# Where the steps of the next layer's modulation stand among the early gate projections

## The chip, the cores and the metric

The kernel runs on one core of a Trainium2 chip. The metric is the device time of one execution in microseconds (us). Engines are named as the profile names them: PE does matrix multiplications (PEld its weight loads), DVE is the vector engine, ACT the scalar engine with its activation functions, POOL the general engine, and SP issues most transfers. Each engine, and each queue of transfers, takes its instructions in one fixed order.

## The reference

A trunk of two layers over 512 tokens of width 1024, all in float32. Each layer:

```python
mod = c_act @ w_ada[l] + b_ada[l]              # 3072 values from one condition vector
shift, scale, gate = split(mod, 3)
h = rms_norm(x, g_pre[l]) * (1 + scale) + shift
cq, ckv, kr, za, qb, kb, vb, zb, qc, kc, vc, zc, gcols = split(h @ w_in[l])
o_a = (mla(cq, ckv, kr) * silu(za)) @ w_o_mla[l]       # low-rank attention, 8 heads
o_b = (swa(qb, kb, vb) * silu(zb)) @ w_o_swa[l]        # sliding window, 8 heads, sinks
o_c = (diff(qc, kc, vc) * silu(zc)) @ w_o_diff[l]      # differential attention, 4 heads
g = sigmoid(gcols)                                     # 3 branches x 1024
y = (g[0] * o_a + g[1] * o_b + g[2] * o_c) @ w_out[l]
x = x + gate * rms_norm(y, g_post[l])
```

The `shift` and `scale` of the second layer depend on the condition vector `c` and on weights alone, so they can be computed at any time during the first layer. They are wanted at the start of the second.

## The kernel before

Activations are kept transposed, with features on the 128 partitions and 512 tokens along the free axis. Every product of two matrices is done as three matmuls: each operand is split into a high part (a copy rounded on ACT) and a low part (the remainder, by a subtraction on DVE), and high x high, low x high and high x low are added up in PSUM. These are lines L87, L88 and L89.

A projection of 128 columns (`proj_T`) takes its weights through `wunit`: one load of 512 KB on SP into a tile `wr` (two buffers; L112), a high part `wh` by ACT (L81, three buffers), a low part `wl` by DVE (L84, three buffers), and then 24 matmuls of 512 columns into a PSUM bank `ps_dn`, of which there are two. A buffer of `wr` is free again once `wl` is written; one of `wh` or `wl` once PE has run the projection.

In the first layer the MLA attention (L769 maxima, L770 exponentials, L774 division on POOL, L703 transposes, L712 to L716 products with the values) is traced first. Behind it stand the early gates: six gate projections of the sliding branch (gb0 to gb5) and five of the differential branch (gc3 to gc7), whose results are put away in DRAM. Then come the keys and values (KB, VB) and four query projections (QB0 to QB3) of the sliding attention, that attention itself (`swa_attention`: L877 and L878 scores, L879 adds the bias and takes the maximum, L883 negates it), and four projections ZB0 to ZB3 (`silu_z`). The program is written with a tile framework: from the traced program and priorities it plans the order of each engine's instructions ahead of time, with a model of their durations. Projections thus run between the pieces of an attention that is waiting. Weight loads get a high priority (`WOFF`).

The next layer's modulation is a generator, `mod_late`. It goes in four quarters, two for `shift` and two for `scale`; each quarter has four steps. One step loads 512 KB of `w_ada` into a `wr` tile on SP (L243) and does two operations of 512 columns on DVE (L246 for the first of a quarter, else L249) that add to an accumulator. With the first step of the next quarter come four small matmuls with a column of ones into a `ps_dn` bank (L255; the trace counts eight) and the reading of the result (L259 for `shift`, L262 and L265 for `scale`).

Who calls it: `some(at)`, with a number for each place. After gate projection gb`j` the number is `j`, after gc`j` it is `8 + j`, and in front of query projection `i` it is `16 + i`. So the calls bear 0, 1, 2, 3, 4, 5, then 11, 12, 13, 14, 15, then 16, 17, 18, 19. A call runs one step if its number is in the tuple `MPOS`, up to eight in all, and the rest of the eight runs in a loop after the queries:

```python
spread = [8]
def some(at):
    table()
    if at in MPOS and spread[0] > 0:
        spread[0] -= 1
        next(late, None)
...
gates_early(l, hh, hl, some)
kk, vb = swa_kv(l, hh, hl)
qs = swa_q(l, hh, hl, some)
while spread[0] > 0:
    some(MPOS[0])
```

`table()` sends one transfer of the bias tables (L445, L451) per call, as long as there are any. The last eight steps of the sixteen are left to `background`, which runs one at a time behind the ZB projections and the gates of the first merge; `mod_rows` (L227 to L233) follows them. In the second layer there is no next layer, and `late` is empty.

Of the kernel before, what the change touches and what calls it, by code (L numbers as in the profile page):

```python
# [50 lines left out]
def hybrid_kernel(ctx, tc, x, c, w_ada, b_ada, g_pre, g_post, w_in, g_q, w_uq, g_kv, w_ukv,  # L51
# [445 lines left out]
    NC_LATE = 3  # L497
    FN = 1

    MPOS = (5, 6, 7, 8, 9, 10, 11, 12)  # L500
    ZBS = 1

    def gates_early(l, hh, hl, some):
# [565 lines left out]
    def rest_of_layer(l, hh, hl, acc, za):  # L1069
# [37 lines left out]
        def table():  # L1107
            if tables:
                try:
                    tables[0].send(units[-1])  # L1110
                except StopIteration:
                    tables.clear()
# [6 lines that stand above are left out]
# [5 lines left out]
        while spread[0] > 0:  # L1124
            some(MPOS[0])
        for _ in range(12):
# [92 lines left out]
```

## Time and profile before

| what | before |
| --- | --- |
| median of three runs | 1199.34 us (1199.33 to 1200.34) |
| the profiled execution | 1196.62 us |
| its span, first to last instruction | 1194.7 us |
| mean granted clock of PE | 0.993 |
| PE busy | 1165.4 us (98%), 5428 matmuls |
| DVE busy | 845.8 us (71%) |
| ACT busy | 632.2 us (53%) |
| POOL busy | 179.3 us (15%) |
| moved by transfers | 146.86 MB, mean 123 GB/s |

A row of the timeline gives the start and the length in us, engine, line and operation, the output and inputs by their names in the program, their shape, a count where rows are merged, and in brackets how long the engine had been idle and what ended that. A matmul's length overlaps the next one's start; the step between two starts is what it costs. Windows are stretches of the span in us; a row gives the busy time of each engine, the granted clock (1.00 is full), the share of the transfer engines' time, and GB/s.

### The profile page before, as it was taken

What the parts mean: (1) busy time and instruction counts of PE and PEld (TensorE: products, weight loads), DVE (VectorE), ACT (ScalarE), POOL (GpSimd) and SP (SyncE); (2) the same over time, 40 slices, a digit from 0 to 9 for tenths busy, and PEclk for the clock granted to TensorE, in tenths of its full rate; (3) what the DMA queues carried; (4) which work ended last, traced back from release to release, by engine and by line L of the source; (5) the groups of instructions that cost most, each with busy time, mean ns of one, the idle gap of its engine ahead of it and who ended that gap; (6) DMA issues with size and microseconds to landing.
All of it is one profiled execution on the core that took longest, in us unless ns stands there. A gap on an engine that the chain in (4) does not pass through costs nothing.

```text
span 1194.7 us, 15536 instructions
## 1 busy us (share of the span) xinstructions
PE 1165.4 (98%) x5428; PEld 947.0 (79%) x5428; DVE 845.8 (71%) x1754; ACT 632.2 (53%) x1250; POOL 179.3 (15%) x226
## 2 busy tenths in 40 slices
PE   5799999999999999999999999999999999999997
PEld 4678788878887888888888888888888888888886
DVE  7956676998865687766577557688785468776554
ACT  5454464655543457654357446565555345665432
POOL 3410212111210010102111001122121001010120
PEclk9899999999999999999999999999999999999999
DMA  9637532255355332443454433224433433334442
GB/s 316 211 86 219 177 111 69 77 158 169 100 155 158 98 86 80 114 120 109 151 174 135 110 102 84 74 66 122 139 102 84 106 86 89 86 101 111 133 161 86
DMA packets 169522, 146.86 MB, mean 123 GB/s; under 512 B 7679, under 2 KB 146999, under 8 KB 169444
## 3 DMA queue, kind: packets, MB, share of 16 engines
q1 hardware_dynamic: 166148, 140.08, 40.7%
q10 hardware_dynamic: 3168, 5.77, 1.4%
q8 instruction: 43, 0.70, 0.2%
q14 instruction: 35, 0.29, 0.1%
q0 software_dynamic: 128, 0.01, 0.0%
HBM read 135.83 MB, written 14.20 MB: 126 GB/s over the span
## 4 chain that ended last, share of the span: by engine, by line
PE 85%; DVE 5%; DMA 4%; issue 2%; ACT 1%; POOL 1%; SPq 1%; DVEq 0%; POOLq 0%; ACTq 0%
PE ps_dn L87 20%; PE ps_dn L88 19%; PE ps_dn L89 19%; PE ps_tr L703 5%; PE ps_sc L89 2%; PE ps_sc L87 2%; PE ps_sc L88 2%; DMA wr<-in_w_in 1%; PE ps_av L712 1%; PE ps_av L713 1%; DMA wr<-in_w_ada 1%; DVE o L204 1%; PE ps_sc L951 1%; PE ps_sc L952 1%; PE ps_pj L87 1%
## 5 line engine op out<-in xcount | busy, mean ns | idle before, releaser
L87 PE MATMUL ps_dn<-hTh,wh 128*128 128x512 f32 x840 | 335.8, 400 | 0.9 <-DVE zz L478 0.7
L89 PE MATMUL ps_dn<-hTh,wl 128*128 128x512 f32 x840 | 334.3, 398 | 0.5 <-DVE wl L84 0.5
L88 PE MATMUL ps_dn<-hTl,wh 128*128 128x512 f32 x840 | 334.0, 398 | 0.0
L84 DVE TENSOR_TENSOR wl<-wr,wh 128x1024 fp32r<-128x1024 f32 x141 | 179.1, 1271 | 104.4 <-ACT wh L81 103.5
L81 ACT ACTIVATE wh<-wr 128x1024 fp32r<-128x1024 f32 x141 | 149.1, 1058 | 174.8 <-PE ps_dn L88 122.2
L89 PEld LDWEIGHTS ps_dn<-hTh,wl 128*128 128x128 f32 x840 | 157.8, 188 | 37.4 <-DVE wl L84 1.0
L87 PEld LDWEIGHTS ps_dn<-hTh,wh 128*128 128x128 f32 x840 | 158.0, 188 | 37.1 <-DVE zz L478 0.9
L88 PEld LDWEIGHTS ps_dn<-hTl,wh 128*128 128x128 f32 x840 | 158.0, 188 | 35.6
L81 ACT ACTIVATE pt<-ps_tr 128x512 fp32r<-128x512 f32 x136 | 78.8, 595 | 69.1 <-PE ps_tr L703 67.8
L84 DVE TENSOR_TENSOR pt<-ps_tr,pt 128x512 fp32r<-128x512 f32 x136 | 92.3, 685 | 32.4 <-ACT pt L81 31.4
L774 POOL TENSOR_SCALAR p<-p,st 128x512 f32<-128x512 f32 x64 | 51.0, 814 | 285.0 <-DVE st L772 230.4
L703 PE MATMUL ps_tr<-ident,p 128*128 128x128 f32 x544 | 92.1, 273 | 0.2
L703 PEld LDWEIGHTS ps_tr<-ident,p 128*128 128x128 f32 x544 | 69.8, 141 | 19.4 <-POOL p L774 0.7
L89 PE MATMUL ps_dn<-u,wl 128*128 128x512 f32 x192 | 76.7, 400 | 0.0
L87 PE MATMUL ps_dn<-u,wh 128*128 128x512 f32 x192 | 76.7, 400 | 0.0
L88 PE MATMUL ps_dn<-u,wh 128*128 128x512 f32 x192 | 76.1, 396 | 0.0
L962 POOL TENSOR_SCALAR ta<-ta,st 128x512 f32<-128x512 f32 x32 | 26.6, 833 | 313.8 <-DVE st L961 132.4
L893 POOL TENSOR_SCALAR p<-p,st 128x256 f32<-128x256 f32 (+1 forms) x64 | 41.2, 662 | 160.6 <-DVE st L891 105.6
L769 DVE TENSOR_REDUCE st<-ps_sc 128x1 f32<-128x512 f32 x64 | 43.5, 687 | 22.2 <-PE ps_sc L89 21.6
L770 ACT ACTIVATE p<-ps_sc,st 128x512 f32<-128x512 f32 x64 | 43.7, 685 | 28.1 <-DVE st L769 27.8
L885 ACT ACTIVATE p<-p,st 128x256 f32<-128x256 f32 (+1 forms) x64 | 35.6, 556 | 20.6 <-DVE st L883 19.8
L958 ACT ACTIVATE p<-p,st 128x512 f32<-128x512 f32 x32 | 23.1, 723 | 37.9 <-DVE st L956 37.8
(345 smaller groups left out, 2107.9 us busy)
## 6 DMA issues: line engine op xcount, KB each, us to landing
wr<-in_w_in SPq DMA_DIRECT2D x105, 512.0 KB, 3.9
wr<-in_w_ada SPq DMA_DIRECT2D x32, 512.0 KB, 3.7
wr<-in_w_out SPq DMA_DIRECT2D x16, 512.0 KB, 3.6
big<-in_w_ada SPq DMA_DIRECT2D x10, 512.0 KB, 9.6
big<-in_x SPq DMA_DIRECT2D x8, 512.0 KB, 5.0
wr<-in_w_o_mla SPq DMA_DIRECT2D x8, 512.0 KB, 3.6
wr<-in_w_o_swa SPq DMA_DIRECT2D x8, 512.0 KB, 3.6
wr<-in_w_o_diff SPq DMA_DIRECT2D x8, 512.0 KB, 3.7
```

The source lines that it names most:

```text
L81: return act.activation(out=out_, in_=in_, func=AF.Copy, scale=scale)
L84: return (eng or dve).tensor_tensor(out=out_, in0=a, in1=b, op=ALU.subtract)
L87: pe.matmul(o, ah, bh, start=start, stop=False)
L88: pe.matmul(o, ah, bl, start=False, stop=False)
L89: pe.matmul(o, al, bh, start=False, stop=stop)
L703: pe.transpose(tr[:, i * P:(i + 1) * P], b, ident)
L769: dve.tensor_reduce(out=nm[:, t:t + 1], in_=s, axis=AX.X, op=ALU.max, negate=True)
L770: act.activation(out=pr[:, t], in_=s, func=AF.Exp, bias=nm[:, t:t + 1], accum_out=sm[:, t:t + 1])
L774: pool.tensor_scalar(out=pr[:, t], in0=pr[:, t], scalar1=rr[:, t:t + 1], scalar2=1.0, op0=ALU.mult, op1=ALU.mult)
L885: act.activation(out=pr[:, i, :w], in_=pr[:, i, :w], func=AF.Exp, bias=nm[:, i:i + 1], accum_out=sm[:, i:i + 1])
L893: pool.tensor_scalar(out=pr[:, i, :w], in0=pr[:, i, :w], scalar1=rr[:, i:i + 1], scalar2=1.0, op0=ALU.mult, op1=ALU.mult)
L962: pool.tensor_scalar(out=pc[1], in0=pc[1], scalar1=rr[:, 1:2], scalar2=1.0, op0=ALU.mult, op1=ALU.mult)
```

## The change

The tuple of places is another one. Nothing else differs.

```diff
-    MPOS = (5, 6, 7, 8, 9, 10, 11, 12)
+    MPOS = (3, 4, 5, 11, 12, 13, 14, 15)
```

Of the old tuple the calls reach 5, 11 and 12, so three steps run among the early gates and five in the loop after the queries. Of the new one the calls reach all eight numbers, so a step stands behind each of gb3, gb4, gb5, gc3, gc4, gc5, gc6 and gc7, and the loop has nothing left to run.

## The prediction

> **What bounds the kernel now.** I read the page's shares first, then a table of windows laid over the stage that the change touches and over everything behind it.
>
> ```profile
> span 1194.7 us, 15536 instructions
> ...
> 95.00:125.00 30.00, 30.00 (x130) 24.20 (x130) 19.03 (x33) 14.54 (x27) 0.00 (x0) 1.00 0.68 203
> 125.00:213.00 88.00, 87.81 (x425) 70.29 (x424) 61.59 (x100) 50.25 (x106) 18.84 (x24) 1.00 0.37 109
> 213.00:245.00 32.00, 32.00 (x157) 25.67 (x156) 31.39 (x51) 18.92 (x37) 7.78 (x8) 1.00 0.35 100
> 245.00:255.00 10.00, 8.09 (x42) 6.32 (x41) 9.63 (x22) 6.70 (x15) 0.00 (x0) 0.83 0.59 161
> 255.00:620.00 365.00, 364.81 (x1694) 296.36 (x1693) 260.99 (x553) 188.75 (x346) 47.44 (x61) 1.00 0.44 127
> 620.00:1180.00 560.00, 559.96 (x2619) 456.43 (x2618) 388.73 (x797) 303.57 (x601) 76.06 (x97) 1.00 0.37 105
> ```
>
> Columns are window, length, then busy time and count of PE, PEld, DVE, ACT and POOL, the granted clock, the DMA share, GB/s. PE never stops from 95 us on, but for 0.2 us in 125:213 and 1.9 us in 245:255, where the clock is down to 0.83 as well. What is not in that one hole is matrix work in a row, so the time changes only by the holes that PE loses or gains. In front of the hole, in 213:245, DVE is busy for 31.39 of 32 us.
>
> Next the hole itself, in PE's timeline and in fine windows.
>
> ```profile
> 246.34 0.60 PE L703 MATMUL ps_tr<-ident,p 128*128 128x128 f32 x4
> 246.78 0.95 PE L255 MATMUL ps_dn<-ones,u 128*128 128x1 f32 x8
> 247.59 0.63 PE L703 MATMUL ps_tr<-ident,p 128*128 128x128 f32 x4
> 249.25 0.39 PE L877 MATMUL ps_sc<-op,op 128*128 128x256 f32 x1 [1.02 <-DVE st L879]
> 249.94 0.33 PE L878 MATMUL ps_sc<-op,op 128*128 128x384 f32 x1
> 251.15 0.79 PE L712 MATMUL ps_av<-pt,big 128*128 128x512 f32 x1 [0.88 <-DVE st L883]
> 251.74 0.63 PE L713 MATMUL ps_av<-pt,big 128*64 128x512 f32 x1
> 253.02 1.05 PE L703 MATMUL ps_tr<-ident,p 128*128 128x128 f32 x4
> 253.73 0.66 PE L87 MATMUL ps_dn<-hTh,wh 128*128 128x512 f32 x1
> 254.22 0.39 PE L88 MATMUL ps_dn<-hTl,wh 128*128 128x512 f32 x1
> ...
> 248.00:250.00 2.00, 0.97 (x7) 0.59 (x4) 1.93 (x7) 0.00 (x0) 0.00 (x0) 1.00 1.02 262
> 250.00:252.00 2.00, 1.12 (x4) 0.65 (x3) 1.97 (x7) 1.44 (x2) 0.00 (x0) 0.68 0.80 240
> 252.00:254.00 2.00, 2.00 (x8) 1.50 (x8) 2.00 (x4) 1.89 (x6) 0.00 (x0) 0.50 0.03 9
> ...
> 135.13 0.23 PE ps_dn L89
> ```
>
> The last row, from the chain of waits, is the undisturbed step of a 512-column matmul, 0.23 us. Between the starts at 247.59 and 254.22 lie 6.63 us. The work in them at full pace: two sets of four transposes, 0.44 us each (246.34 to 246.78), two 256-column and two 384-column score matmuls (0.12 and 0.17 each by their columns, 0.58), five 512-column ones (1.15): 2.6 us. The hole is worth 6.6 - 2.6 = 4.0 us. Of that some 2.3 us are the two waits for DVE (247.59 + 0.44 to 249.25 is 1.2; 249.94 + 0.17 to 251.15 is 1.0), the other 1.7 us slow matmuls at a clock of 0.68 and 0.50.
>
> The Trainium skill (TensorE: Matmul & The Clock Gate, "What's actually happening") says that the clock is halved after an idle window of some 3.4 us. By that the two short waits would not have slowed anything, and only their 2.3 us could come back; the rows disagree, since the clock falls right behind waits of 1.0 and 0.9 us.
>
> Why nothing filled the hole is seen on the queue of loads (SP), on DVE, and in what the first ZB projection needs.
>
> ```profile
> 198.45 0.37 SPq L112 DMA_DIRECT2D wr<-in_w_in  x1
> ...
> 213.66 10.39 SPq L243 DMA_DIRECT2D wr<-in_w_ada  x3
> ...
> 231.08 6.01 SPq L243 DMA_DIRECT2D wr<-in_w_ada  x2
> 240.04 0.37 SPq L112 DMA_DIRECT2D wr<-in_w_in  x1
> ...
> 245.45 1.23 DVE L84 TENSOR_TENSOR wl<-wr,wh 128x1024 fp32r<-128x1024 f32 x1
> ...
> 247.52 0.49 DVE L246 TENSOR_SCALAR big<-wr,cact 128x512 f32<-128x512 f32 x1
> 248.04 0.75 DVE L249 SCALAR_TENSOR_TENSOR big<-wr,cact,big 128x512 f32<-128x512 f32 x1
> 248.71 0.48 DVE L879 CUSTOM_DVE_ANT_0 p<-ps_sc,x,sinkt 128x256 f32<-128x256 f32 x1
> ...
> 251.68 0.14 DVE L259 TENSOR_TENSOR ashf<-ps_dn,prT 128x4 f32<-128x4 f32 x1
> ```
>
> Counting the loads into `wr` from gb0 on, they leave in program order: 198.45 is the last query weight (QB3), then come the five steps, and ZB0 only at 240.04. ZB0 is split at 245.45 and could run from 246.7, but its `ps_dn` bank (two in all) is held by the sums of step five (L255 at 246.78), read by L259 at 251.68 behind the DVE backlog. Meanwhile L879, which PE waits for, stands on DVE behind 1.2 us of a further step.
>
> **The change, part by part.** The calls carry the numbers 0 to 5, 11 to 15 and 16 to 19. Today 5, 11 and 12 match; the other five steps run in the loop behind the query projections. With the new tuple 3, 4, 5 and 11 to 15 match: eight steps, and the loop runs no more. Instructions, bytes and loads stay the same; the second layer has no such steps. The tables of the bias are all sent by call 16 either way. Five steps move, each with one 512 KB load on SP, two DVE operations and two waits; the sums L255 and L259 of the first quarter go with step five, to call 12. On SP they pass the weight loads of gates and queries, the bias tables, one pair of attention weights and four bias loads. On POOL's queue and ACT's nothing of theirs stands.
>
> (a) Leaving 213:245. What the steps do on DVE there, in windows of L249 and of L246 alone:
>
> ```profile
> 213.00:245.00 32.00, 7.38 (x9) 1.00 0.35 100
> ...
> 213.00:245.00 32.00, 0.48 (x1) 1.00 0.35 100
> ```
>
> Nine of L249 and one of L246, 7.9 us of the 31.4 that DVE works there. ZB0 takes the slot of the load at 213.66, some 26 us sooner, and a `ps_dn` bank directly behind the queries, with the sums gone. Not all of the 7.9 us is relief: the background steps behind ZB0 and ZB1 move up with their loads, about two into this window (2 x 1.4 us), and a split of 1.23 us. That leaves 7.9 - 2.8 - 1.2 = 3.9 us. L879 and what follows it on DVE were late by the 1.0 and 0.9 us that PE waited; 3.9 us covers both. And ZB0's 24 matmuls (24 x 0.23 = 5.6 us) are there to run whenever L879 is late all the same. I take the whole hole as gone: -4.0 us; bounds 0 and -4.4 (the hole and the 0.2 us each that PE is idle in 125:213 and 255:620).
>
> (b) Arriving in 95:150. What is late next is the start of the MLA attention, whose rows are
>
> ```profile
> 105.04 1.06 ACT L81 ACTIVATE wh<-wr 128x1024 fp32r<-128x1024 f32 x1 [3.63 <-PE ps_dn L88]
> 106.47 0.49 DVE L246 TENSOR_SCALAR u<-wr,cact 128x512 f32<-128x512 f32 x1 [4.42 <-DMA wr<-in_w_ada]
> 112.04 1.06 ACT L81 ACTIVATE wh<-wr 128x1024 fp32r<-128x1024 f32 x1 [1.78 <-PE ps_dn L88]
> 120.74 1.06 ACT L81 ACTIVATE wh<-wr 128x1024 fp32r<-128x1024 f32 x1 [0.24 <-DMA wr<-in_w_in]
> 123.22 1.54 DVE L249 SCALAR_TENSOR_TENSOR u<-wr,cact,u 128x512 f32<-128x512 f32 x2 [1.90 <-DMA wr<-in_w_ada]
> ...
> 130.55 3.75 POOL p L774 x4
> ...
> 134.34 0.55 PE ps_tr L703 x3
> ...
> wr<-in_w_ada SPq DMA_DIRECT2D x3, 512.0 KB, 5.4
> ```
>
> The last row is that of the loads from 95 to 135. Each step keeps one of two `wr` slots for 5.4 us of load and 1.3 us of DVE, 6.7 us. I followed the two slots by hand in the new order gb3, s3, gb4, s4, gb5, s5, gc3, s11, gc4, s12: gb4's load stays near 98 but in the other slot, gb5's goes from 98.0 to some 105, gc3's from 107.8 to some 113, gc4's from 116.3 to some 121. Splits of gb5 and gc3 waited for PE to free `wh` (3.63 and 1.78 us), not for loads, and with three `wh` buffers a split runs about two gates (2 x 5.6 us) ahead of its use: a delay of 5 to 7 us fits under that cover of 11 us. Were the cover gone, PE would wait by the difference. The later steps take slots that stood full waiting for PE; KB, VB and the queries keep their times by the same count.
>
> DVE has room (19.03 of 30 us busy in 95:125), but its queue is in order: a step whose load is late holds what stands behind it (at 106.47 for 4.42 us, at 123.22 for 1.90 us), that is the splits, the copies of keys and the maxima of the first head. Behind those wait the POOL divisions at 130.55 and PE's transposes at 134.34, where PE's 0.2 us of idle lie. So today's three steps cost PE 0.2 us, the nearest row; the far bound, two more steps in front of the first softmax, is 2 x (4.42 + 1.24) = 11.3 us less a gate of 5.6 us in the gap, 5.7 us. I take +0.6 us, three times the row for eight steps in place of three, rounded.
>
> The Trainium skill (DMA: Bandwidth & Descriptors, "Queues, rings and completion order") says that what one queue row sends is consumed in ring order; by it a step's load in front of a gate's delays it by its whole transfer, as the 5.4 us beside table writes would agree. It speaks for the far bound of 5.7 us and not for 0.6.
>
> (c) The sums of the first quarter between gc4 and gc5: eight matmuls, 0.8 us (246.78 to 247.59), on PE wherever they stand: 0, or a wait for their bank of under the 0.6 us of one tanh.
>
> Sum: -4.0 + 0.6 = -3.4 us. The profiled execution took 1196.62 us, span 1194.7 and 1.9 around it, so it would be 1193.2; it stands 2.7 us below the median of the runs shown, 1199.34, and on that the sum gives 1195.9 us.
>
> **The rivals.** (1) The hole shrinks but stays. For it: L879 stood right behind a background step, and those move up too; DVE had only 3.9 us to gain in a window with 0.6 us free. Against it: ZB0 as filler. If one of the two waits remains with its slow clock, half of 4.0 comes back, and with 0.6 spent the time is 1197.9. An order of instructions, rebuilt by the planner, that loses elsewhere what it wins belongs here too. (2) Slower: the start of MLA. s3 and s4 hold DVE in front of the first head and PE's fixed order runs out of gates between 105 and 140. At the far bound of 5.7 us with 1.7 us of slow clock behind it, less the 4.0 won, it ends at 1202.7; it decides from a stall of 6.4 us on (4.0 + 2.4). For it: the chain of waits runs through these very rows. Against it: PE is at 30.00 of 30. (3) The slow clock isn't owed to the waits: the 1.7 us stay, and -2.3 + 0.6 gives 1197.6. The rows 248 to 254 speak against it, where the clock is 1.00, 0.68, 0.50 in turn. It is what the Trainium skill's page on TensorE, quoted above, would make of the hole. (4) No effect: ZB0's load was hidden anyway, 1199.3. PE's two waits speak against it.
>
> **How the numbers follow.** About 0.2%, 2.4 us, is what a measurement can tell from no change. The forecast, hole gone and start nearly free, 0.54: 1194.9 to 1196.9. Rival 1, 0.21, rival 3, 0.03, and rival 4, 0.07, fall within 0.2%. Rival 2, 0.15. The likeliest gives 1195.9. The range runs from 1194.4 (bound of -4.4 and half a us for the 1.0 us between the runs shown) to 1201.7, where the slower case begins.
>
> **What would show it.** Right: PE in the window of the old hole full and the clock 1.00; ZB0's load directly behind QB3's near 214; no L243 rows between the queries and ZB0; L255 on `u` near 145. Wrong: a new gap of PE between 100 and 140 with a DVE wait on `in_w_ada` in front of it, the waits on L879 and L883 still there, or PE idle at a new place past 255.

## The result and the profile after

The changed kernel is slower by about as much as a measurement can tell. Its median is 1201.26 us (1200.01 to 1203.33, ten runs) against 1199.12 us for the kernel before in the same session; the ratio is 1.0025, with an interval of 1.0016 to 1.0034. A later session gave 1197.18 against 1195.77, ratio 1.0016 (1.0007 to 1.0024). The prediction was 1195.9 us: it had the sign wrong.

The profiled execution took 1203.29 us, 2.0 above its median, while that of before lies 2.5 below the median of its ten. The two traces thus differ by 6.5 us where the medians differ by 2.1, so below I compare stretches, not spans. First the windows of the changed kernel, in the stretches of the prediction:

```profile
span 1201.2 us, 15547 instructions
...
95.00:125.00 30.00, 30.00 (x131) 24.19 (x130) 20.79 (x34) 14.16 (x28) 0.00 (x0) 1.00 0.76 226
125.00:213.00 88.00, 84.69 (x404) 67.10 (x403) 65.05 (x107) 48.16 (x101) 19.58 (x24) 1.00 0.46 134
213.00:245.00 32.00, 32.00 (x162) 25.65 (x161) 27.32 (x42) 20.97 (x41) 6.99 (x8) 1.00 0.26 72
245.00:255.00 10.00, 10.00 (x54) 8.21 (x53) 8.35 (x17) 6.42 (x13) 0.00 (x0) 1.00 0.40 106
255.00:620.00 365.00, 362.73 (x1672) 293.76 (x1671) 256.31 (x547) 185.22 (x339) 46.82 (x59) 1.00 0.43 121
```

The old hole is gone: PE is busy for 10.00 of 10 us in 245:255, where it had 8.09 at a clock of 0.83. DVE in 213:245 fell from 31.39 to 27.32 us, 4.1 us of relief where 3.9 were predicted (the steps there shrank by 5.6 us, other work grew by 1.5). But 125:213 lost 3.1 us of PE (87.81 to 84.69), and 255:620 lost 2.1 (364.81 to 362.73). Two new holes took the place of one.

The loads moved as said, those of the gates within 2 us and ZB0's some 6 us later than the 214 named. In the queue of loads of the changed kernel ZB0's weights (219.56) leave directly behind the last query's (204.34), with no step between:

```profile
204.34 0.37 SPq L112 DMA_DIRECT2D wr<-in_w_in  x1
219.56 0.38 SPq L112 DMA_DIRECT2D wr<-in_w_in  x1
227.97 0.38 SPq L243 DMA_DIRECT2D wr<-in_w_ada  x1
```

The first new hole lies in the first heads of the MLA attention. These are the timelines of DVE, POOL and PE of the changed kernel there; the bracket gives how long the engine stood idle and what ended it:

```profile
131.31 0.74 DVE L249 SCALAR_TENSOR_TENSOR u<-wr,cact,u 128x512 f32<-128x512 f32 x1
132.07 0.69 DVE L769 TENSOR_REDUCE st<-ps_sc 128x1 f32<-128x512 f32 x1
136.02 1.93 DVE L249 SCALAR_TENSOR_TENSOR u<-wr,cact,u 128x512 f32<-128x512 f32 x2 [0.18 <-DMA wr<-in_w_ada]
153.62 1.54 DVE L249 SCALAR_TENSOR_TENSOR u<-wr,cact,u 128x512 f32<-128x512 f32 x2 [3.38 <-DMA wr<-in_w_ada]
155.07 0.68 DVE L769 TENSOR_REDUCE st<-ps_sc 128x1 f32<-128x512 f32 x1
162.56 0.15 DVE L259 TENSOR_TENSOR ashf<-ps_dn,prT 128x4 f32<-128x4 f32 x1
...
133.90 4.61 POOL L774 TENSOR_SCALAR p<-p,st 128x512 f32<-128x512 f32 x4 [57.31 <-DVE st L772]
...
136.36 0.44 PE L703 MATMUL ps_tr<-ident,p 128*128 128x128 f32 x2 [0.85 <-POOL p L774]
137.46 0.44 PE L703 MATMUL ps_tr<-ident,p 128*128 128x128 f32 x2 [0.43 <-POOL p L774]
138.56 0.44 PE L703 MATMUL ps_tr<-ident,p 128*128 128x128 f32 x2 [0.42 <-POOL p L774]
155.01 0.72 PE L255 MATMUL ps_dn<-ones,u 128*128 128x1 f32 x6
156.62 0.50 PE L87 MATMUL ps_sc<-op,op 128*128 128x512 f32 x1 [0.89 <-ACT p L770]
160.31 0.51 PE L87 MATMUL ps_dn<-hTh,wh 128*128 128x512 f32 x1 [0.60 <-ACT tf L491]
```

Three things are to be seen. (i) Between 136 and 139 the transposes run at POOL's pace. The divisions start at 133.90 (130.55 before): the reciprocal on DVE that starts them (L772) leads PE's first transposes by 1.29 us (133.61 to 134.90), where it led by 2.95 before (130.27 to 133.22). And they take 4.61 us for four (3.74 before), while DVE does two L249 of a step at the same time, in 1.93 us (two alone took 1.54). (ii) At 153.62 a step's load has kept DVE idle for 3.38 us. The maximum L769 behind it is late, then the exponential (ACT L770), then the scores at 156.62. (iii) The sums L255 take a `ps_dn` bank at 155.01 and it is read only at 162.56, because L259 stands behind all this on DVE. With one bank left, the next gate projection at 160.31 has to wait until the last one's tanh (L491) has read it, and that tanh itself runs only at 159.66 on ACT, behind the late exponential.

The second new hole lies in the sliding attention, 10 to 40 us behind the old one:

```profile
262.00:268.00 6.00, 5.15 (x29) 4.29 (x29) 4.98 (x14) 4.42 (x9) 1.30 (x2) 1.00 0.56 150
284.00:294.00 10.00, 8.93 (x45) 7.10 (x44) 6.68 (x22) 5.01 (x10) 2.28 (x4) 0.85 0.55 154
...
265.35 0.50 PE L87 MATMUL ps_dn<-hTh,wh 128*128 128x512 f32 x1 [0.85 <-DVE ashf L259]
288.96 0.38 PE L877 MATMUL ps_sc<-op,op 128*128 128x256 f32 x1 [0.30 <-DVE st L879]
290.63 0.45 PE L715 MATMUL ps_av<-pt,big 128*64 128x512 f32 x1 [0.77 <-DVE st L883]
...
283.61 0.37 SPq L243 DMA_DIRECT2D wr<-in_w_ada  x1
...
287.75 0.75 DVE L249 SCALAR_TENSOR_TENSOR big<-wr,cact,big 128x512 f32<-128x512 f32 x1 [3.29 <-DMA wr<-in_w_ada]
288.42 0.48 DVE L879 CUSTOM_DVE_ANT_0 p<-ps_sc,x,sinkt 128x256 f32<-128x256 f32 x1
```

At 265 PE waits for the bank that the second quarter's sums hold. At 287.75 a background step waits 3.29 us for its load, issued at 283.61, with L879 behind it on DVE, and PE waits for L879 and L883 as it did in the old hole, again at a lower clock (0.85, and 0.50 in 292:294).

To compare kernels I worked out a **loss** from the starts in PE's timeline: the distance between each two starts, less an undisturbed step (0.2335 us for 512 columns and in proportion, 0.11 for a transpose, 0.1 for a one-column matmul), added up by stretches. Unlike busy time it counts slow matmuls too. In us:

| kernel | 95:130 | 130:170 | 170:245 | 245:310 | ratio to before (95%) |
| --- | --- | --- | --- | --- | --- |
| before | -0.1 | 0.4 | 0.2 | 3.9 | 1 |
| changed | -0.1 | 4.7 | -0.5 | 3.9 | 1.0025 (1.0016 to 1.0034) |
| changed, later session (f4) | 0.0 | 4.1 | -0.4 | 1.4 | 1.0016 (1.0007 to 1.0024) |
| e1: steps at 3, 4, 5, 11, 12, three in the loop | -0.1 | 0.7 | -0.4 | 4.3 | 1.0001 (0.9993 to 1.0010) |
| e2: 5, 11, 12, 15 to 19 | -0.1 | 0.0 | 0.5 | 0.0 | 0.9968 (0.9956 to 0.9981) |
| e3: changed, no loads for the eight steps | 0.3 | -0.2 | -0.2 | 1.0 | 1.0048 (1.0034 to 1.0062) |
| e4: changed, little DVE work in them | -0.1 | 0.5 | -0.3 | 1.2 | 0.9968 (0.9955 to 0.9980) |
| f1: 3, 4, 5, 11, 12, 17, 18, 19 | -0.1 | 1.1 | 0.0 | 0.0 | 0.9975 (0.9965 to 0.9985) |
| f2: 5, 11 to 15, 18, 19 | -0.1 | 1.6 | 0.5 | 1.3 | 0.9995 (0.9987 to 1.0004) |
| f3: before, sums in another bank | -0.1 | -0.2 | -0.3 | 0.9 | 0.9972 (0.9962 to 0.9982) |
| g1: changed, sums in another bank | -0.1 | 2.5 | 0.1 | 0.0 | 0.9981 (0.9972 to 0.9990) |
| g2: e2, sums in another bank | -0.1 | 0.4 | -0.2 | 0.1 | 0.9969 (0.9958 to 0.9981) |
| h1: changed, one step with little DVE work | -0.1 | 4.8 | -0.5 | 2.9 | 1.0028 (1.0017 to 1.0040) |

The losses are of one profiled execution each, and good to about half a us. Those of the changed kernel in 245:310 (3.9 and 1.4) show how far two executions can be apart: the order of its instructions is the same in both, but in f4 the clock stayed at 1.00, which is some 1.5 of the 2.5 us, and two of the three waits were shorter or absent. Ahead of 95 us the losses scatter by some 2 us between executions (only e3, below, has a reason of its own).

### The profile page after: what moved, and what is told of

Its sections match the earlier page's. It is cut to its first block, busy times and chain, and to the rows that moved or that the text cites. A ratio compares the mean times of both kernels' runs of the same rounds, so it can differ in the third digit from the quotient of the medians.

```text
span 1201.2 us, 15547 instructions
## 1 busy us (share of the span) xinstructions
PE 1169.1 (97%) x5428; PEld 948.7 (79%) x5428; DVE 844.5 (70%) x1754; ACT 632.0 (53%) x1250; POOL 180.2 (15%) x226
## 4 chain that ended last, share of the span: by engine, by line
PE 77%; DVE 10%; DMA 8%; ACT 2%; issue 2%; POOL 0%; SPq 0%; DVEq 0%; POOLq 0%; ACTq 0%
PE ps_dn L87 18%; PE ps_dn L88 18%; PE ps_dn L89 18%; PE ps_tr L703 4%; DMA wr<-in_w_ada 3%; DMA wr<-in_w_in 3%; DVE o L204 2%; PE ps_sc L87 2%; PE ps_sc L89 2%; PE ps_sc L88 2%; DVE wl L84 2%; PE ps_sc L952 1%; PE ps_sc L951 1%; PE ps_av L713 1%; PE ps_av L712 1%
## 5 line engine op out<-in xcount | busy, mean ns | idle before, releaser
L84 DVE TENSOR_TENSOR wl<-wr,wh 128x1024 fp32r<-128x1024 f32 x141 | 179.5, 1274 | 110.0 <-ACT wh L81 109.3
L84 DVE TENSOR_TENSOR pt<-ps_tr,pt 128x512 fp32r<-128x512 f32 x136 | 92.2, 685 | 29.1 <-ACT pt L81 28.2
L774 POOL TENSOR_SCALAR p<-p,st 128x512 f32<-128x512 f32 x64 | 51.0, 817 | 285.2 <-DVE st L772 259.4
L770 ACT ACTIVATE p<-ps_sc,st 128x512 f32<-128x512 f32 x64 | 43.8, 686 | 36.1 <-DVE st L769 34.0
L769 DVE TENSOR_REDUCE st<-ps_sc 128x1 f32<-128x512 f32 x64 | 43.4, 686 | 14.8 <-PE ps_sc L89 14.4
```

The costliest lines, as they stand in the source:

```text
L84: return (eng or dve).tensor_tensor(out=out_, in0=a, in1=b, op=ALU.subtract)
L769: dve.tensor_reduce(out=nm[:, t:t + 1], in_=s, axis=AX.X, op=ALU.max, negate=True)
L770: act.activation(out=pr[:, t], in_=s, func=AF.Exp, bias=nm[:, t:t + 1], accum_out=sm[:, t:t + 1])
L774: pool.tensor_scalar(out=pr[:, t], in0=pr[:, t], scalar1=rr[:, t:t + 1], scalar2=1.0, op0=ALU.mult, op1=ALU.mult)
```

## The experiments

**Where the steps stand.** Two kernels with other places, e1 and e2, and two with the places of the change but without loads, or almost without DVE work. My theory then: the waits for late loads on DVE make the early hole, three steps too many among the gates make the rest.

```diff
-    MPOS = (5, 6, 7, 8, 9, 10, 11, 12)
+    MPOS = (3, 4, 5, 11, 12)                     # e1
+    MPOS = (5, 11, 12, 15, 16, 17, 18, 19)       # e2
```

> Five steps among the first gates (behind gb3, gb4, gb5, gc3, gc4), none behind gc5 to gc7, three in the loop behind the queries. Late loads on the in-order DVE queue at the start of the MLA attention (first theory): PE's hole between 130 and 140 us is there, 2 us or more over the kernel before; the one between 150 and 165, which belongs to the steps behind gc6 and gc7, is gone; the time is 1199.5 to 1201.5. DVE work of the steps (rival): the same here. A mere accident of the planned order (second rival): no tie between the places of the steps and the holes, a time anywhere from 1196 to 1203.

Measured: 1196.03 us against 1196.09, ratio 1.0001, faster than the 1199.5 us from which my theory started; the hole of 2 us between 130 and 140 did not come. Two steps more at gb3 and gb4, with none behind gc5 to gc7, cost next to nothing in 130:170 (0.4 to 0.7). Three steps left in the loop keep a hole of the old one's size (3.9 and 4.3), some 8 us later:

```profile
245.00:262.00 17.00, 14.97 (x75) 12.02 (x74) 14.02 (x32) 8.48 (x19) 0.00 (x0) 0.92 0.52 156
```

So s3 and s4 by themselves, which the prediction's rival 2 blamed, do not stop PE.

> The three early steps of the kernel before (5, 11, 12), the other five behind gc7 and in front of each query projection (15 to 19), none in the loop. First theory: PE's idle time between 95 and 165 us is back to that of the kernel before (under 1 us), and the hole ahead of or in the sliding attention is 2 to 4 us; 1197 to 1199.5. Rival, DVE work: the steps now add their DVE work in 190 to 235 us, where DVE is busiest with the queries, so the hole of 245 to 255 of the kernel before stays at 4 us and the time is 1199 or more. Accident: anything.

Measured: 1192.86 us, ratio 0.9968, faster than any of the forecasts with a figure. Both holes are gone:

```profile
245.00:262.00 17.00, 17.00 (x88) 14.03 (x87) 14.75 (x34) 8.12 (x17) 1.87 (x4) 1.00 0.46 141
262.00:300.00 38.00, 38.00 (x195) 31.53 (x194) 28.86 (x82) 21.59 (x49) 7.21 (x13) 1.00 0.44 132
```

The aim of the change, to clear the place ahead of the sliding attention, is worth 3 to 4 us (3.2 by the medians, 3.8 by the ratio) if most of the moved steps go in front of the queries in place of the first heads.

```diff
+                if q < 2:
+                    src = [rq, rq]
+                else:
                     raw = T("wr", [P, 2, S])
                     sp.dma_start(out=raw, in_=w_ada[l]...)
+                    src = [raw[:, 0], raw[:, 1]]
```

> The changed kernel, but the eight spread steps read a resident tile (the rope table) and load nothing; their DVE operations stay as they are. Left out: the loads of the next layer's shift weights. First theory (waits for late loads): the holes between 130 and 165 us shrink from 4.6 us of lost PE time to under 1.5, and the time falls by 3 us or more, to 1198 or less. Rival (DVE work): the holes stay at 3 us or more, time within 1.5 us of the changed kernel's 1201.3.

Measured: 1202.13 us, and not for the reason under test. Without a load to wait for, the planner moved the eight steps' DVE work to 51 to 72 us, into the input stage of the layer, and there PE stood still:

```profile
53.09 1.41 DVE L253 SCALAR_TENSOR_TENSOR u<-rq,cact,u 128x512 f32<-128x512 f32 x2
...
71.15 0.74 DVE L253 SCALAR_TENSOR_TENSOR u<-rq,cact,u 128x512 f32<-128x512 f32 x1
...
72.22 0.71 PE L87 MATMUL ps_sc<-u,hTh 128*128 128x416 f32 x1 [7.88 <-ACT hTh L81]
```

The run says nothing on load waits. It does show that 95:245 runs without a hole when no step is in it.

```diff
+                    n = 64 if q < 2 else S
-                    dve.scalar_tensor_tensor(out=acc, in0=raw[:, i], ...
+                    dve.scalar_tensor_tensor(out=acc[:, 0:n], in0=raw[:, i, 0:n], ...
```

> The changed kernel, but of the eight spread steps all DVE operations after a quarter's first work on 64 of 512 columns; the loads and the waits for them stay. Left out: seven eighths of the sum of the next layer's shift. First theory: holes between 130 and 165 us stay at 3 us or more, time within 1.5 us of 1201.3. Rival (DVE work): they shrink to under 1.5 us and the time falls to 1198 or less.

Measured: 1192.35 us, ratio 0.9968. Loads, waits and places are those of the change. DVE still waits for them, here for 2.78 us with maxima behind it, and PE is full:

```profile
148.44 0.61 DVE L250 SCALAR_TENSOR_TENSOR u<-wr,cact,u 128x64 f32<-128x64 f32 x2 [2.78 <-DMA wr<-in_w_ada]
...
152.00:162.00 10.00, 10.00 (x52) 8.19 (x51) 9.49 (x17) 6.34 (x14) 2.86 (x4) 1.00 0.56 155
```

The waits of DVE in 130:170 add up to 5.0 us here, the same as in the changed kernel. So late loads alone don't make the hole, and my theory falls in that form. As I read it, the work of the L249 is needed as well, because it makes the queue behind a wait too long to be caught up. But with the shorter work the planner also chose another order (on PE from 107 us on), so the run separates neither the work from the order nor the work of one step from that of another.

**Which of the eight steps.**

```diff
+    MPOS = (3, 4, 5, 11, 12, 17, 18, 19)         # f1
+    MPOS = (5, 11, 12, 13, 14, 15, 18, 19)       # f2
```

> Five steps among the first gates as in the kernel that moved five early (3, 4, 5, 11, 12), the other three in front of query projections (17, 18, 19), none behind gc5 to gc7 and none in the loop. Theory now: a hole has two makers, the steps behind gc5 to gc7 (13 to 15), which hold DVE in the first heads of the MLA attention, and the five or three steps of the loop, which hold it ahead of the sliding attention; this kernel has neither. PE loses under 1 us in 130 to 170 us and under 1.5 us in 245 to 310; 3 to 4 us faster than the kernel before (ratio 0.997). Rival (the steps behind gb3 and gb4 hurt): 2 us or more lost before 170 us. Rival (accident of the order): either hole may be there.

> The other half: steps behind gb5, gc3 to gc7 (5, 11 to 15) and two in front of queries (18, 19); no steps behind gb3 and gb4, none in the loop. Theory now: the three steps at 13 to 15 cost PE 2 to 4.7 us between 130 and 170 us as in the changed kernel, and since PE then runs late against the planned order of DVE, a second hole of 2 to 4 us comes in the sliding attention at 245 to 310; the time is that of the kernel before or 0.3% above it. Rival (it took gb3 and gb4 as well, that is eight steps between 95 and 150): no hole before 170 us, and the time is 3 us below the kernel before.

Measured: f1 1192.82 us, ratio 0.9975, and f2 1195.09 us, ratio 0.9995. f1 is the changed kernel with three steps taken from behind gc5, gc6 and gc7 to the fronts of the last three queries, and this alone is worth 4.4 us: the changed kernel, run again in the same session (f4 below), took 1197.18 us. Up to the L249 of the first of these steps, at 136 us, PE, DVE, ACT and POOL have the same order of instructions in both. The first heads of f1:

```profile
131.32 3.74 POOL L774 TENSOR_SCALAR p<-p,st 128x512 f32<-128x512 f32 x4 [56.24 <-DVE st L772]
...
133.78 0.44 PE L703 MATMUL ps_tr<-ident,p 128*128 128x128 f32 x2 [0.69 <-POOL p L774]
...
151.57 0.95 PE L255 MATMUL ps_dn<-ones,u 128*128 128x1 f32 x8
...
154.07 0.15 DVE L259 TENSOR_TENSOR ashf<-ps_dn,prT 128x4 f32<-128x4 f32 x1
```

POOL is back at 3.74 us, one of three waits is left, and the sums hold their bank for 2.5 us (151.57 to 154.07) in place of 7.6.

f2 missed its forecast: it keeps the steps behind gc5, gc6 and gc7, and its loss in 130:170 is 1.6 us, not 2 to 4.7, and 1.3 in 245:310, not 2 to 4. Its rows there are

```profile
130.00:142.00 12.00, 11.30 (x56) 8.98 (x55) 8.25 (x12) 4.10 (x10) 4.11 (x4) 1.00 0.49 162
152.00:162.00 10.00, 9.78 (x47) 7.55 (x46) 9.53 (x17) 7.45 (x15) 1.95 (x3) 1.00 0.50 143
```

So the early hole is owed neither to the three steps alone (f2) nor to s3 and s4 alone (e1, f1): taking away either group removes most of it. Where s3 and s4 are in, the reciprocal L772 has a shorter lead over PE's first transposes: 2.95, 3.20 and 3.12 us without them (before, e2, f2), 1.29, 1.28, 1.84 and 1.44 with them (changed, f4, e1, f1; g1 below is an exception). f2 also takes its first sums at 178 us, away from the first heads, so it is not a test of the steps alone.

By the number of steps between 95 and 150 us, the loss in 130:170 goes 3 steps 0.4 (before), 4 steps 0.0 (e2), 5 steps 0.7 and 1.1, 6 steps 1.6, 8 steps 4.1 and 4.7: the last ones cost far more than the first.

**The bank.** Step (a) of the prediction said that the old hole hung on the bank that the sums held. f3 is the kernel before with that alone changed in the program; `pj` is the bank of the attention's projections. f4 is the changed kernel again, beside it.

```diff
-            pst = Q("dn")
+            pst = Q("pj")
```

> The kernel before, with the small sums of each quarter (L255) in the bank that the transposes of the values use (pj) instead of one of the two projection banks. If the bank keeps ZB0 from filling the hole of 245 to 255 us, as the prediction said, the hole falls from 3.9 us to under 2 and the kernel is 2 us faster. If it is the DVE backlog left by the five steps alone, the hole stays at 3 us or more and the time with it.

> The changed kernel once more, beside the others on their chip: 0.25% slower than before, with 3 us or more lost in 130 to 170 us and 3 us or more in 245 to 310. If the early loss is an accident of one execution (loads that landed late once), it is under 2 us here.

Measured: f3 1192.80 us, ratio 0.9972; f4 1197.18 us, ratio 1.0016. Not one step is moved in f3, though the planner's order changes with the edit, on PE from 231 us on. The old hole is gone:

```profile
245.00:262.00 17.00, 17.00 (x92) 14.19 (x92) 15.06 (x39) 8.26 (x18) 2.37 (x4) 1.00 0.57 162
262.00:300.00 38.00, 37.42 (x191) 30.63 (x189) 31.48 (x86) 23.25 (x54) 7.15 (x12) 1.00 0.57 172
...
247.04 0.16 DVE L259 TENSOR_TENSOR ashf<-ps_pj,prT 128x4 f32<-128x4 f32 x1
247.12 0.48 DVE L879 CUSTOM_DVE_ANT_0 p<-ps_sc,x,sinkt 128x256 f32<-128x256 f32 x1
```

The old hole was made by a bank as much as by five steps in a row. ZB0's load was not what held it: it leaves at 239.17 in f3, behind the same five steps (240.04 before), and ZB0 runs in the place of the old hole. f4 repeats the first new hole in full and the second in part:

```profile
132.22 4.60 POOL L774 TENSOR_SCALAR p<-p,st 128x512 f32<-128x512 f32 x4 [56.62 <-DVE st L772]
...
134.07 2.19 DVE L249 SCALAR_TENSOR_TENSOR u<-wr,cact,u 128x512 f32<-128x512 f32 x2
...
146.15 2.70 POOL L774 TENSOR_SCALAR p<-p,st 128x512 f32<-128x512 f32 x4 [9.33 <-DVE st L772]
...
262.00:300.00 38.00, 36.92 (x186) 30.25 (x185) 29.70 (x83) 21.14 (x50) 8.32 (x12) 1.00 0.47 144
```

The same edit in the changed kernel and in e2:

> The changed kernel, with the sums L255 in the bank of the attention's projections (`ps_pj`) in place of one of the two `ps_dn` banks. Theory: the bank held by the sums from 155 to 162.6 makes the waits `ps_dn [0.60 <-ACT tf L491]` at 160.3 and `ps_dn [0.85 <-DVE ashf L259]` at 265.4; with it gone the loss of PE starts in 130 to 170 falls from 4.1 to 4.7 us to about 3, and that in 245 to 310 stays under 1.5. The first half of the early hole, where the transposes wait for POOL's divisions at 136 to 138, stays at about 2.4 us. Time 1 to 2.5 us under the changed kernel's, ratio to the kernel before 1.000 (0.999 to 1.001). Rival: the early hole is owed to the bank alone; then nothing over 1 us is lost in 130 to 170 and the ratio is 0.997. Second rival: `ps_pj` has one buffer, which the attention's rotations use; they wait instead, and the time stays that of the changed kernel, 1.0016 to 1.0025.

> The eight steps at 5, 11, 12 and 15 to 19 (the version with one step behind each query), and the sums in `ps_pj` as well. That version already loses nothing in 95 to 310 beyond 0.5 us, so the bank has nothing to give: ratio 0.9965 to 0.9975, the same as without it. Rival: the two edits free different holes and add; then 0.995 or lower.

Measured: g1 1193.86 us against 1196.02, ratio 0.9981; g2 1192.35 us, ratio 0.9969. In g1 the planner put the first quarter's sums at 218 and later, far from the first heads, and what is left of the early hole is about half:

```profile
130.00:142.00 12.00, 11.28 (x54) 8.75 (x54) 8.54 (x11) 5.34 (x10) 4.12 (x4) 1.00 0.61 187
...
152.00:162.00 10.00, 9.03 (x44) 6.98 (x43) 8.91 (x16) 7.39 (x15) 0.17 (x1) 1.00 0.43 122
...
262.00:300.00 38.00, 38.00 (x196) 31.45 (x195) 29.74 (x84) 20.60 (x48) 7.46 (x12) 1.00 0.44 130
```

The bank, with the order that follows from it, is 0.0035 to 0.0044 of the time in the changed kernel, 4 to 5 us, more than the 1 to 2.5 us expected: the second new hole (0.0 in 245:310) goes with it. Two of the transposes' three waits are absent too, but that can't be the order: on PE, DVE and POOL it is that of the changed kernel up to 155 us. In this execution the reciprocal L772 led PE's first transposes by 2.63 us in place of 1.29; why it did is not shown. With the bank out of the way in both, the change goes from 0.9972 (f3) to 0.9981 (g1); the intervals overlap, so what the moved steps cost by themselves is about 1 us or nothing. g2 gives no more than e2, as expected: where no hole is left, the bank has nothing to give.

**POOL beside DVE.** h1 shrinks one step's DVE work, the two L249 that run beside POOL's divisions; the order of the instructions up to that place is unchanged, while behind it the planner's order is another one (on PE from 140 us on).

```diff
+    def mod_late(l, N=lambda q, k: 64 if (q, k) == (1, 2) else S):
...
+                    dve.scalar_tensor_tensor(out=acc[:, 0:N(q, k)], ...
```

> The changed kernel, with the two L249 of one step (the one at 13, at 134 to 138 us) on 64 of 512 columns: a part of the next layer's shift is left out. Its load, its wait and its place stay. Theory: those two L249 run beside POOL's four divisions and stretch them from 3.74 to 4.60 us, and PE's transposes wait for POOL; without them POOL takes 3.7 to 3.9 us, two of the three waits on L774 go, and the loss in 130 to 170 falls by 1 to 2.4 us; the second half, at 155 to 160, stays. Ratio 1.000 to 1.0015. Rival: POOL's divisions are slow for another reason, or PE waits because the divisions start late; then POOL stays at 4.6 us or the three waits stay, and the loss is that of the changed kernel, 4.0 to 4.7 us.

Measured: 1198.87 us, ratio 1.0028. POOL does what the theory says, and the time does not:

```profile
133.74 3.75 POOL L774 TENSOR_SCALAR p<-p,st 128x512 f32<-128x512 f32 x4 [57.26 <-DVE st L772]
...
135.60 1.30 DVE L249 SCALAR_TENSOR_TENSOR u<-wr,cact,u 128x64 f32<-128x64 f32 x2
...
130.00:142.00 12.00, 10.76 (x48) 7.75 (x47) 8.26 (x13) 6.02 (x13) 3.75 (x4) 1.00 0.73 236
152.00:162.00 10.00, 7.99 (x42) 6.20 (x41) 7.68 (x13) 6.03 (x12) 0.00 (x0) 1.00 0.30 89
```

Four divisions take 3.75 us, and the waits of 0.43 and 0.42 us are gone. PE gains 0.6 us in 130:142 (10.18 to 10.76) and loses 0.5 of it again in 152:162 (8.52 to 7.99), where the step's load is late as before. So the stretching of POOL is real, and undoing it wins nothing here: the loss in 130:170 is 4.8 us, as in the changed kernel. That the late steps behind it open the gap again is how I read it; since the order behind 140 us differs, the run doesn't show it.

## Why the prediction was wrong

**What bounds the kernel, and (a).** Right in its reading of most of the old hole: it was worth some 4 us, the `ps_dn` bank held by the sums stood behind it (f3 takes the bank away, ratio 0.9972, without moving a step), the relief of DVE was 4.1 us for 3.9, and all of that hole went. ZB0's load, the other cause named, was not needed for it: it leaves as late as before in f3. But "I take the whole hole as gone: -4.0 us" was wrong for the stretch. Steps, sums and the bank did not go away; the background steps and the second quarter's sums moved up behind ZB0's load, and 1.4 to 3.9 us were lost again at 262 to 292. So the term was between 0.0 and -2.5 us. That is the last sentence of rival 1, an order that loses elsewhere what it wins, but rival 1 was priced by half of the hole left at its old place. The -4.0 was to be had with some of the steps in front of queries (e2, f1), or with this tuple and the sums in another bank (g1): there the same stretch loses nothing.

**(b)** is the term that was furthest off. It gave +0.6 us; the loss in 130:170 rose by 3.7 to 4.3 us. The slot chain was right, and so was the cover of the gates: 95:130 loses nothing. What was wrong is to let the later steps rest on that chain ("The later steps take slots that stood full waiting for PE"): I counted these steps as loads only. Their DVE operations and their waits land among the maxima of the first heads, where PE's fixed order has one gate matmul for each pair of transposes (136 to 139 us) and then stands behind DVE. f1 and f2 together show that it takes both groups, s3 and s4 in front and the steps behind gc5, gc6 and gc7: without the latter the loss is 1.1 us, without the former 1.6. "Three times the row for eight steps in place of three" took a cost for proportional that is not: 0.4 us at three steps became 0.7 to 1.1 at five and 4.1 to 4.7 at eight. How much of it is DVE's work and how much the planned order is open.

**(c)** "0, or a wait for their bank under the 0.6 us of one tanh": there is a wait of 0.60 us at 160.31, just that tanh, which is luck. The bound took the bank as free after one read, and the read L259 stands on DVE behind the steps; the bank was held for 7.6 us. The second quarter's sums cost another 0.85 us at 265. g1 prices the bank at 4 to 5 us in this kernel, with the order that it brings. So (b) and (c) can't be set apart wholly: with another bank 2.5 us of the early loss stay, and the second new hole goes.

**The signs.** Of those named for being right, L255 came at 155.01 and not near 145. Two of those named for being wrong came: PE idle between 100 and 140 with late steps on DVE in front, and PE idle at a new place past 255.

**The rivals.** Rival 2 gave 1202.7 us, and the outcome was nearest to it, in part by its mechanism: with s3 and s4 in front of the first head the divisions lose about half of their lead over PE (g1 excepted), and PE waits for POOL at 136. But PE is full to 130 us, no stall of 5.7 us is there, and without the steps behind gc5 to gc7 little comes of it (e1, f1). The rule of the Trainium skill that spoke for that bound (DMA: Bandwidth & Descriptors, "Queues, rings and completion order") has descriptors consumed in ring order. No run here tests it: gc4's load left at 119.65 us in place of 116.27, as the count of slots had it. Rival 3 had the slow clock stay at the old hole; there the clock is 1.00 in the changed kernel, so it fell. But what lowers the clock is open. It fell to 0.50 behind waits of PE of 0.30 and 0.77 us (changed, 292:294) and of 0.74, 0.65 and 0.63 us (e1, 260:262), and stayed at 1.00 behind one of 0.77 us in f4 and ones of 1.36 and 1.20 us in h1. All of them are short of the idle window of some 3.4 us that the Trainium skill gives (TensorE: Matmul & The Clock Gate, "What's actually happening"). So the 1.7 us of slow clock in the -4.0 may be in one execution and not in another. Rival 4's time, no change, lies just outside the measured interval (1.0016 to 1.0034); its premise, that ZB0's load was hidden, is borne out by f3.

**The sum.** Forecast -3.4 us, measured +2.1 (first session) and +1.4 to +1.9 (later session, by the medians and by the ratio). By the loss of the later profiled execution, (b) at +3.7 and (a) at -2.5 give +1.2; by the first, +4.3 and 0.0 give +4.3; the measured values lie between.

**Left open.** Why DVE waits 1.88 and 3.29 us for background loads at 276 to 288 in the changed kernel, and only 1.52 and 1.16 us at 270 to 281 in f1, without harm there, is not settled, since the planner's order differs. Whether the kernel before has the slow clock in every execution is not known, as one was profiled. Nor was a third buffer for `wr` tried, or a tile of their own for the steps' loads.

## What to carry to other kernels

A piece of side work that is spread out must be followed on every engine's queue to the place where it lands, not only through its load slots: late loads with in-order work behind them cost nothing beside full projections and, with the work of eight steps, several us among the first maxima of an attention. If side work borrows a PSUM bank from a pool of two, price the time until its reader runs, behind everything queued ahead of it, and try another pool first: here that one word won as much as the best new set of places. Costs of extra steps don't add up in proportion; test a dose (three, five, six, eight), and each group of steps without the other, before multiplying a row.

## What the runs showed of the hardware

Operations of DVE with two inputs in SBUF and divisions on POOL (L774, 128x512) slow each other when they run at once. Beside DVE work that takes an input from PSUM, four divisions take 2.70 us (f4 at 146.15). The 3.74 us of the first four in the kernel before hold one of 1.73 us that runs beside a weight split (L84, `wl` from `wr` and `wh`); the other three take 0.69 us each. In the changed kernel the L249 of a step come beside them as well: two divisions take 1.12 us each and the four 4.61 (4.60 in its repeat, 4.12 in g1, where the divisions meet the split and the L249 at other moments), and two L249 take 1.93, 2.19 and 2.28 us in place of 1.54. With the two L249 cut to 64 columns, POOL was back at 3.75 us, and the short ones themselves took 1.30 us in place of 0.61 (h1 against e4). The prediction has no term for this. The Trainium skill has a rule for it (SBUF — State Buffer, "Who interferes with whom"): a DVE instruction with two SBUF inputs contends with a GpSimd instruction that reads SBUF, and the ports that they share are an exclusive lock. The runs agree that both sides are slowed. But if each L249 had kept POOL out for its whole 0.77 us, a division beside it would have taken 0.69 + 0.77 = 1.46 us by this estimate; it took 1.12.
